# One tile, one copy and one subtraction for the silu products of both token tiles in the FFNs of a decoder trunk

## The chip, the cores and the metric

The kernel runs on one core of one Trainium2 chip. Its time is the device time of one execution in microseconds, and a kernel's time is the median over its runs. A profile shows one execution, taken by the hardware profiler.

## The reference

A decoder trunk of two layers over 256 tokens of width 1024, all in float32. Each layer has two SwiGLU FFNs with 2816 hidden columns, a pair of token mixers between them, three layer norms, and a gated embedding (PLE) at the end:

```python
def swiglu(x, w_gate, w_up, w_down):
    return (jax.nn.silu(x @ w_gate) * (x @ w_up)) @ w_down

def reference(x, p, ...):
    for i in range(DEPTH):
        x = layer_norm(DN_ALPHA * x + 0.5 * swiglu(x, ffn_w_gate[i, 0], ffn_w_up[i, 0], ffn_w_down[i, 0]),
                       ln_g[i, 0], ln_b[i, 0])
        if i % 2 == 0:
            mix = mixer_ab(...)
        else:
            mix = mixer_cd(...)
        x = layer_norm(DN_ALPHA * x + mix, ln_g[i, 1], ln_b[i, 1])
        x = layer_norm(DN_ALPHA * x + 0.5 * swiglu(x, ffn_w_gate[i, 1], ffn_w_up[i, 1], ffn_w_down[i, 1]),
                       ln_g[i, 2], ln_b[i, 2])
        x = x + jax.nn.sigmoid(x @ ple_w_gate[i]) * (p[i] @ ple_w_proj[i])
    return x
```

## The kernel before

The 256 tokens are two tiles (`NT`) of 128. The FFNs are called f00 and f01 (layer 0) and f10 and f11 (layer 1). Behind f00 come layer norm 0, mixer_ab (its first projection writes `pj_u`) and layer norm 1; behind f01 layer norm 2 and PLE0, then f10; behind f10 layer norm 3 and mixer_cd (first projection `pj_hq`); behind f11 layer norm 5 and PLE1, which ends the kernel.

Every product is split: an operand is held as a rounded part (`...h`, type fp32r) and a remainder (`...l`), and `mm3` (L70, L71, L72) issues three matmuls, wh with xh, wl with xh, wh with xl. So weights pass through three steps: SyncE loads a unit of 1 MB into `wst`, ScalarE casts half of it to `wh` (L61), VectorE subtracts to get `wl` (L62). An activation that changes from tokens-by-features to features-by-tokens is transposed by TensorE into PSUM (tag `tr`, two buffers), cast by ScalarE and subtracted by VectorE: `xh` and `xl` (L112, L113) for layer norms and PLE, `hh` and `hl` (L212, L213) inside the FFN.

An FFN goes through 11 slices of 256 hidden columns. `gate_up(f)` is 48 matmuls into two PSUM tiles `gu`, one for each token tile; `hidden(f)` makes silu(gate) times up (`sg`, L205 and L206), transposes it (`ht`, L209) and splits it; `down(f)` is 24 matmuls into four accumulators `acc_<FFN>_<token tile>_<half of 1024 columns>`. The down matmuls of slices 9 and 10 stand in a last loop over the token tiles, with the layer norm of the tile right behind its own:

```python
    for t in range(NT):
        for n in range(2):
            for f in (NF - 2, NF - 1):
                down(f, t, hs[f], ds[f], (n,))
        layer_norm(g, ln, t, acc[t], 0.5 / ALPHA, xT)
```

`layer_norm` is a chain on VectorE: L126 (`r_ln`, a half of 512 columns at a time) with statistics behind each half, small operations, L136 and L138 (`x_ln`) by halves; then TensorE transposes (`tp_ln`, L142) and `xh`, `xl` follow. PLE's projection (`pps`, copied to `pp`) needs no layer norm; its gate (`acc_ple`) does. During f00 hooks prepare S5 parameters (`s5w`, `s5k` through `tr`, `s5pe` copies at L546, L553 and L558). At the end of f00 ScalarE's queue also issues the loads of mixer_ab: `nw_dt` (L593, cast at L597), `abrow` (L764), and W, tab, T, Q from `s5d` (L671 to L677), twice. At the end of f10 it issues `nw_glr` (L593, cast at L597) and `gup`.

The program names dependencies, not an order. Tile's scheduler (`schedule_with_timeline_sim=True`) lays out the order of each engine's instructions with a cost model of its own; `behind` adds an edge that keeps one instruction after another on the same engine.

Of the kernel before, what the change touches and what calls it, by code (L numbers as in the profile page):

```python
# [33 lines left out]
def f32(ap):  # L34
    return ap.bitcast(F32)
# [81 lines left out]
def layer_norm(g, n, t, acc, coef, xT):  # L117

    nc = g.nc
    name = f"ln{n}_{t}"  # L120
    r = g.lnp.tile([P, D], F32, tag="ln_r", name=f"r_{name}")
    st = g.small.tile([P, 2, 6], F32, tag="ln_st", name=f"st_{name}")
    half = [slice(512 * h, 512 * h + 512) for h in range(2)]
    for h in range(2):
        s = half[h]
        op = nc.vector.scalar_tensor_tensor(r[:, s], acc[h], coef, g.x[t][:, s], op0=ALU.mult, op1=ALU.add)  # L126
        if t:
            behind(g, op, g.scaled)
        nc.vector.bn_stats(st[:, h, :], r[:, s])
    mv = g.small.tile([P, 2], F32, tag="ln_mv", name=f"mv_{name}")  # L130
    nc.vector.bn_aggr(mv, st.rearrange("p a b -> p (a b)"))
    rstd = rsqrt(g, mv[:, 1:2], 1, EPS / (ALPHA * ALPHA), 1.0, name)
    x = g.xp.tile([P, D], F32, tag=f"x{t}", name=f"x_{name}")
    for h in range(2):
        s = half[h]
        nc.vector.scalar_tensor_tensor(r[:, s], r[:, s], mv[:, 0:1], g.grow[n][0][:, s], op0=ALU.subtract,  # L136
                                       op1=ALU.mult)
        op = nc.vector.scalar_tensor_tensor(x[:, s], r[:, s], rstd, g.grow[n][1][:, s], op0=ALU.mult, op1=ALU.add)  # L138
        g.scaled = (op.ins,)
        tp = g.ps.tile([P, 4, P], F32, tag="tr", name=f"tp_{name}_{h}", bufs=2)  # L140
# [17 lines left out]
def acc_tiles(g, name):  # L158
    return [[g.ps.tile([P, 512], F32, tag="acc", name=f"acc_{name}_{t}_{h}", bufs=4) for h in range(2)]
            for t in range(NT)]  # L160


def run_tiles(g, ps, xT, tile_major=False):

    nc = g.nc

    def part(kh, t, pieces):
        for j in range(4):
            k = 4 * kh + j
            wh, wl = pieces[j // 2]  # L170
            c = slice(512 * (j % 2), 512 * (j % 2) + 512)
            mm3(nc, ps[t], *of_tile(xT, t, k), wh[:, c], wl[:, c], k == 0, k == KT - 1)

    if tile_major:
        units = [g.w.unit() for kh in range(2)]
        for t in range(NT):
            for kh in range(2):
                part(kh, t, units[kh])
        return
    for kh in range(2):  # L180
        pieces = g.w.unit()
        for t in range(NT):
            part(kh, t, pieces)
# [8 lines left out]
def ffn_body(g, name, ln, hooks, hp, wx):  # L192
    nc = g.nc
    acc = acc_tiles(g, name)

    def gate_up(f):
        ps = [g.ps.tile([P, 512], F32, tag="mm", name=f"gu_{name}_{f}_{t}", bufs=2) for t in range(NT)]
        run_tiles(g, ps, g.xT, tile_major=f == 0)
        return ps

    def hidden(f, ps):
        out = []
        for t in range(NT):
# [12 lines left out]

    def down(f, t, h, pieces, cols=(0, 1)):
        hh, hl = h[t]
        for n in cols:
            for k in range(2):  # L220
                wh, wl = pieces[k]
                c = slice(512 * n, 512 * n + 512)
                mm3(nc, acc[t][n], hh[:, k, :], hl[:, k, :], wh[:, c], wl[:, c],
                    f == 0 and k == 0, f == NF - 1 and k == 1)

    ps = gate_up(0)
    if -1 in hooks:
        hooks[-1]()
    hs, ds = {}, {}
    for f in range(NF):  # L230
        hs[f] = hidden(f, ps)
        if f + 1 < NF:
            ps = gate_up(f + 1)
        for d in DOWNS[f]:
            ds[d] = g.w.unit(wx if d >= NF - 2 else None)
            if d < NF - 2:
                for t in range(NT):
                    down(d, t, hs[d], ds[d])
        if f in hooks:
            hooks[f]()  # L240
    xT = new_xT(g, f"{name}")
# [5 lines that stand above are left out]
    g.xT = xT  # L247
# [1270 lines left out]
```

## Time and profile before

| | |
|---|---|
| median of 3 runs | 1237.29 us (1236.95 to 1238.12) |
| profiled execution, its own time | 1236.71 us |
| its span | 1234.9 us |
| mean granted TensorE clock | 0.996 |
| TensorE busy | 97% of the span |
| VectorE, ScalarE busy | 69%, 50% |

The time of an execution is its span and a little around it. Shares of busy time are averages over the whole span. [...]

### The profile page before, as it was taken

What the parts mean: (1) busy time and instruction counts of PE and PEld (TensorE: products, weight loads), DVE (VectorE), ACT (ScalarE), POOL (GpSimd) and SP (SyncE); (2) the same over time, 40 slices, a digit from 0 to 9 for tenths busy, and PEclk for the clock granted to TensorE, in tenths of its full rate; (3) what the DMA queues carried; (4) which work ended last, traced back from release to release, by engine and by line L of the source; (5) the groups of instructions that cost most, each with busy time, mean ns of one, the idle gap of its engine ahead of it and who ended that gap; (6) DMA issues with size and microseconds to landing.
All of it is one profiled execution on the core that took longest, in us unless ns stands there. A gap on an engine that the chain in (4) does not pass through costs nothing.

```text
span 1234.9 us, 16234 instructions
## 1 busy us (share of the span) xinstructions
PE 1202.8 (97%) x6274; PEld 1011.3 (82%) x6274; DVE 848.5 (69%) x1353; ACT 621.1 (50%) x944; POOL 48.5 (4%) x78
## 2 busy tenths in 40 slices
PE   6999999899999999999999999999999899999998
PEld 4888788699997878888887888887888778888886
DVE  6998874779879876555567554546689776545466
ACT  6566765444535635444536444443575535444434
POOL 0000000020101000000000000000100010000000
PEclk9999999999999999999999999999999999999999
DMA  7676778687842647555535655554633227555532
GB/s 267 218 253 241 248 259 320 219 289 263 278 140 72 222 143 254 177 198 180 195 137 204 217 192 186 189 190 165 227 122 137 103 80 255 185 193 182 197 144 102
DMA packets 40797, 242.12 MB, mean 196 GB/s; under 512 B 4848, under 2 KB 5520, under 8 KB 17040
## 3 DMA queue, kind: packets, MB, share of 16 engines
q1 hardware_dynamic: 30672, 206.06, 48.2%
q0 software_dynamic: 3952, 18.88, 4.3%
q10 hardware_dynamic: 6096, 16.16, 3.9%
q8 instruction: 49, 0.80, 0.3%
q14 instruction: 28, 0.23, 0.1%
HBM read 224.30 MB, written 16.78 MB: 195 GB/s over the span
## 4 chain that ended last, share of the span: by engine, by line
PE 72%; issue 5%; DVE 3%; DMA 1%; POOL 0%; ACT 0%; DVEq 0%; ACTq 0%; POOLq 0%
PE gu_f L72 10%; PE gu_f L71 10%; PE gu_f L70 9%; PE acc_f L72 5%; PE acc_f L70 5%; PE acc_f L71 5%; PE acc_ple L71 1%; PE acc_ab L70 1%; PE acc_ab L72 1%; PE acc_ab L71 1%; PE acc_ple L72 1%; PE acc_ple L70 1%; PE ht_f L209 1%; PE lv_h L1140 1%; PE lv_g L1140 1%
## 5 line engine op out<-in xcount | busy, mean ns | idle before, releaser
L62 DVE TENSOR_TENSOR wl<-wst,wh 128x1024 fp32r<-128x1024 f32 (+1 forms) x378 | 453.6, 1216 | 269.2 <-ACT wh L61 262.7
L61 ACT CAST wh<-wst 128x1024 fp32r<-128x1024 f32 (+1 forms) x378 | 386.7, 1045 | 319.8 <-PE gu_f L72 108.0
L70 PE MATMUL acc_f<-wh,hh_f 128*128 128x512 f32 x352 | 137.4, 391 | 1.2 <-ACT hh_f L212 1.2
L71 PE MATMUL acc_f<-wl,hh_f 128*128 128x512 f32 x352 | 137.7, 391 | 0.0
L72 PE MATMUL acc_f<-wh,hl_f 128*128 128x512 f32 x352 | 136.3, 392 | 0.2 <-DVE hl_f L213 0.2
L70 PEld LDWEIGHTS acc_f<-wh,hh_f 128*128 128x128 f32 x352 | 66.1, 188 | 15.4 <-ACT hh_f L212 2.1
L72 PEld LDWEIGHTS acc_f<-wh,hl_f 128*128 128x128 f32 x352 | 66.1, 188 | 14.1 <-DVE hl_f L213 0.7
L71 PEld LDWEIGHTS acc_f<-wl,hh_f 128*128 128x128 f32 x352 | 66.1, 188 | 13.5
L70 PE MATMUL gu_f<-wh,xh_in 128*128 128x512 f32 x176 | 70.9, 408 | 5.9 <-ACT wh L61 5.9
L205 ACT ACTIVATE sg_f<-gu_f 128x256 f32<-128x256 f32 x88 | 33.7, 384 | 75.1 <-PE gu_f L72 73.3
L70 PE MATMUL gu_f<-wh,xh_ple 128*128 128x512 f32 x176 | 69.7, 396 | 1.6 <-ACT xh_ple L112 1.6
L71 PE MATMUL gu_f<-wl,xh_in 128*128 128x512 f32 x176 | 70.7, 403 | 0.0
L70 PE MATMUL gu_f<-wh,xh_cd 128*128 128x512 f32 x176 | 69.8, 396 | 0.5 <-ACT xh_cd L112 0.5
L70 PE MATMUL gu_f<-wh,xh_ab 128*128 128x512 f32 x176 | 69.7, 396 | 0.5 <-ACT xh_ab L112 0.5
L72 PE MATMUL gu_f<-wh,xl_in 128*128 128x512 f32 x176 | 70.1, 399 | 0.0
L72 PE MATMUL gu_f<-wh,xl_ab 128*128 128x512 f32 x176 | 69.0, 392 | 0.7 <-DVE xl_ab L113 0.7
L72 PE MATMUL gu_f<-wh,xl_cd 128*128 128x512 f32 x176 | 69.0, 392 | 0.7 <-DVE xl_cd L113 0.7
L71 PE MATMUL gu_f<-wl,xh_cd 128*128 128x512 f32 x176 | 68.8, 391 | 0.2 <-DVE wl L62 0.2
L71 PE MATMUL gu_f<-wl,xh_ab 128*128 128x512 f32 x176 | 68.8, 391 | 0.2 <-DVE wl L62 0.2
L72 PE MATMUL gu_f<-wh,xl_ple 128*128 128x512 f32 x176 | 68.7, 392 | 0.0
L71 PE MATMUL gu_f<-wl,xh_ple 128*128 128x512 f32 x176 | 68.6, 390 | 0.0
L206 DVE TENSOR_TENSOR sg_f<-sg_f,gu_f 128x256 f32<-128x256 f32 x88 | 36.5, 416 | 27.2 <-ACT sg_f L205 27.2
(470 smaller groups left out, 2397.0 us busy)
## 6 DMA issues: line engine op xcount, KB each, us to landing
wst<-in_wall_dram SPq DMA_DIRECT2D x185, 1024.0 KB, 4.9
s5d<-s5pk POOLq DMA_DIRECT2D x8, 896.0 KB, 4.7
s5d<-s5pe POOLq DMA_DIRECT2D x8, 768.0 KB, 3.8
row<-in_lnr_dram SPq DMA_DIRECT2D x12, 512.0 KB, 6.4
W<-s5d ACTq DMA_DIRECT2D x8, 512.0 KB, 6.5
Q<-s5d ACTq DMA_DIRECT2D x8, 512.0 KB, 5.5
tab<-s5d ACTq DMA_DIRECT2D x8, 384.0 KB, 3.8
wst<-in_wall_dram SPq DMA_DIRECT2D x4, 512.0 KB, 6.4
```

The source lines that it names most:

```text
L61: ops = [nc.scalar.copy(wh[:, c], src[:, c])]
L62: ops.append(nc.vector.tensor_tensor(wl[:, c], src[:, c], f32(wh[:, c]), op=ALU.subtract))
L70: nc.tensor.matmul(out, xh, wh, start=first, stop=False)
L71: nc.tensor.matmul(out, xh, wl, start=False, stop=False)
L72: nc.tensor.matmul(out, xl, wh, start=False, stop=last)
L205: nc.scalar.activation(sg, ps[t][:, 0:256], AF.Silu)
L206: nc.vector.tensor_tensor(sg, sg, ps[t][:, 256:512], op=ALU.mult)
L209: nc.tensor.transpose(tp[:, k, :], sg[:, k * P:(k + 1) * P], g.ident)
L1140: nc.tensor.matmul(lp[0:m, n * t + j], xt[:, 0:m], xt.rearrange("p (a s b) -> p a s b", s=2, b=b)[:, :, 1, :], start=True, stop=True)
```

## The change

`hidden` holds both token tiles in one tile each: `sg` [128, 2, 256] with one buffer (it was one tile for each token tile, two buffers), `ht` [128, 2, 2, 128] in one `tr` buffer (it was one for each token tile), and `hh`, `hl` with three buffers as before. The two silu activations and the two products still go token tile by token tile. The four transposes follow in a fixed order, tile 1 first; one cast and one subtraction over 512 columns split all of it. `down` is as it was, on slices of the new tiles. `g.hidden` is used nowhere else. In the changed kernel lines behind L201 have numbers higher by up to 3 (L207 for L205, L215 for the cast and subtraction).

```diff
--- before.py
+++ after.py
@@ -199,20 +199,22 @@
         return ps
 
     def hidden(f, ps):
-        out = []
+        sg = hp.tile([P, NT, 256], F32, tag="sg", name=f"sg_{name}_{f}", bufs=1)
+        tp = g.ps.tile([P, NT, 2, P], F32, tag="tr", name=f"ht_{name}_{f}", bufs=2)
+        hh = hp.tile([P, NT, 2, P], F32R, tag="hh", name=f"hh_{name}_{f}", bufs=3)
+        hl = hp.tile([P, NT, 2, P], F32R, tag="hl", name=f"hl_{name}_{f}", bufs=3)
         for t in range(NT):
-            sg = hp.tile([P, 256], F32, tag="sg", name=f"sg_{name}_{f}_{t}")
-            nc.scalar.activation(sg, ps[t][:, 0:256], AF.Silu)
-            nc.vector.tensor_tensor(sg, sg, ps[t][:, 256:512], op=ALU.mult)
-            tp = g.ps.tile([P, 2, P], F32, tag="tr", name=f"ht_{name}_{f}_{t}", bufs=2)
+            nc.scalar.activation(sg[:, t], ps[t][:, 0:256], AF.Silu)
+            nc.vector.tensor_tensor(sg[:, t], sg[:, t], ps[t][:, 256:512], op=ALU.mult)
+        last = ()
+        for t in reversed(range(NT)):
             for k in range(2):
-                nc.tensor.transpose(tp[:, k, :], sg[:, k * P:(k + 1) * P], g.ident)
-            hh = hp.tile([P, 2, P], F32R, tag=f"hh{t}", name=f"hh_{name}_{f}_{t}", bufs=3)
-            hl = hp.tile([P, 2, P], F32R, tag=f"hl{t}", name=f"hl_{name}_{f}_{t}", bufs=3)
-            nc.scalar.copy(hh, tp)
-            nc.vector.tensor_tensor(hl, tp, f32(hh), op=ALU.subtract)
-            out.append((hh, hl))
-        return out
+                op = nc.tensor.transpose(tp[:, t, k, :], sg[:, t, k * P:(k + 1) * P], g.ident)
+                behind(g, op, last)
+                last = (op.ins,)
+        ops = [nc.scalar.copy(hh, tp), nc.vector.tensor_tensor(hl, tp, f32(hh), op=ALU.subtract)]
+        g.hidden = tuple(op.ins for op in ops)
+        return [(hh[:, t], hl[:, t]) for t in range(NT)]
 
     def down(f, t, h, pieces, cols=(0, 1)):
         hh, hl = h[t]
```

ScalarE and VectorE each have 44 instructions fewer; TensorE has as many as before. The scheduler's order changes in many places. Three of them follow, without the numbers that stand ahead of the rows.

TensorE at the end of f10, the last rows of the FFN before the transposes of layer norm 3. A name is the tile, then FFN, token tile and column half, and `hh_f10_10` is slice 10. Before:

```order
L72 MATMUL acc_f10_1_1_6250<-wh_130_0_7549,hl_f10_9_1_7420 128x512
L70 MATMUL acc_f10_1_1_6250<-wh_130_1_7553,hh_f10_9_1_7419 128x512
L71 MATMUL acc_f10_1_1_6250<-wl_130_1_7554,hh_f10_9_1_7419 128x512
L72 MATMUL acc_f10_1_1_6250<-wh_130_1_7553,hl_f10_9_1_7420 128x512
L70 MATMUL acc_f10_1_1_6250<-wh_131_0_7559,hh_f10_10_1_7509 128x512
L71 MATMUL acc_f10_1_1_6250<-wl_131_0_7560,hh_f10_10_1_7509 128x512
L72 MATMUL acc_f10_1_1_6250<-wh_131_0_7559,hl_f10_10_1_7510 128x512
L70 MATMUL acc_f10_1_1_6250<-wh_131_1_7563,hh_f10_10_1_7509 128x512
L71 MATMUL acc_f10_1_1_6250<-wl_131_1_7564,hh_f10_10_1_7509 128x512
L72 MATMUL acc_f10_1_1_6250<-wh_131_1_7563,hl_f10_10_1_7510 128x512
L142 MATMUL tp_ln3_0_0_7608<-cs_209,x_ln3_0_7605 128x128 x4
L142 MATMUL tp_ln3_0_1_7617<-cs_209,x_ln3_0_7605 128x128 x4
```

After:

```order
L71 MATMUL acc_f10_0_1_6116<-wl_131_1_7366,hh_f10_10_7303 128x512
L72 MATMUL acc_f10_0_1_6116<-wh_131_1_7365,hl_f10_10_7304 128x512
L72 MATMUL acc_f10_1_0_6117<-wh_131_0_7361,hl_f10_10_7304 128x512
L70 MATMUL acc_f10_1_0_6117<-wh_131_1_7365,hh_f10_10_7303 128x512
L71 MATMUL acc_f10_1_0_6117<-wl_131_1_7366,hh_f10_10_7303 128x512
L72 MATMUL acc_f10_1_0_6117<-wh_131_1_7365,hl_f10_10_7304 128x512
L72 MATMUL acc_f10_1_1_6118<-wh_131_0_7361,hl_f10_10_7304 128x512
L70 MATMUL acc_f10_1_1_6118<-wh_131_1_7365,hh_f10_10_7303 128x512
L71 MATMUL acc_f10_1_1_6118<-wl_131_1_7366,hh_f10_10_7303 128x512
L72 MATMUL acc_f10_1_1_6118<-wh_131_1_7365,hl_f10_10_7304 128x512
L142 MATMUL tp_ln3_0_0_7410<-cs_209,x_ln3_0_7407 128x128 x4
L142 MATMUL tp_ln3_0_1_7419<-cs_209,x_ln3_0_7407 128x128 x4
```

Before, the last rows are all of `acc_f10_1_1`, and the last row of token tile 0 stands 24 matmuls ahead of `tp_ln3_0_0`; now slice 10 is run for all four accumulators, and the last row of token tile 0 (`acc_f10_0_1`) stands 8 matmuls ahead of `tp_ln3_0_0`.

ScalarE at the end of f00, from the loads of mixer_ab to the casts of layer norm 0's first token tile (`DMA` rows are issues of transfers). Before:

```order
L593 DMA nw_dt_2423<-in_abdt_dram 128x128
L671 DMA W_0_2448<-s5d0_87 128x1024
L673 DMA tab_0_2450<-s5d0_87 128x768
L597 CAST nws_dt_2425<-nw_dt_2423 128x8x16
L675 DMA T_0_2452<-s5d0_87 128x512
L677 DMA Q_0_2454<-s5d0_87 128x1024
L764 DMA abrow_2499<-in_abrow_dram 128x48
L671 DMA W_1_2528<-s5d1_88 128x1024
L112 CAST xh_f00_2078<-tp_ln0_0_0_2119 128x4x128
L673 DMA tab_1_2530<-s5d1_88 128x768
L112 CAST xh_f00_2078<-tp_ln0_0_1_2128 128x4x128
```

After (the issues of `nw_dt` and `abrow` stand just ahead):

```order
L599 CAST nws_dt_2359<-nw_dt_2357 128x8x16
L774 ACT_TABLE_LOAD
L774 ACTIVATE A_2458<-abrow_2433 128x16
L673 DMA W_0_2382<-s5d0_87 128x1024
L675 DMA tab_0_2384<-s5d0_87 128x768
L677 DMA T_0_2386<-s5d0_87 128x512
L679 DMA Q_0_2388<-s5d0_87 128x1024
L673 DMA W_1_2462<-s5d1_88 128x1024
L675 DMA tab_1_2464<-s5d1_88 128x768
L677 DMA T_1_2466<-s5d1_88 128x512
L679 DMA Q_1_2468<-s5d1_88 128x1024
L112 CAST xh_f00_2012<-tp_ln0_0_0_2053 128x4x128
```

The activation of `abrow` with its table load, which stood seven rows behind the first `xh_f00` cast, and three more of the W, tab, T, Q issues now stand ahead of it.

VectorE at the end of f01, from layer norm 2 of token tile 1 to the subtraction for weight unit 95, PLE0's first. Before:

```order
L126 SCALAR_TENSOR_TENSOR r_ln2_1_5967<-acc_f01_1_0_4568,x_ln1_1_4532 128x512
L126 SCALAR_TENSOR_TENSOR r_ln2_1_5967<-acc_f01_1_1_4569,x_ln1_1_4532 128x512
L129 BN_STATS st_ln2_1_5968<-r_ln2_1_5967 128x6 x2
L131 BN_AGGR mv_ln2_1_5973<-st_ln2_1_5968 128x2
L79 TENSOR_SCALAR rs_w_ln2_1_5975<-mv_ln2_1_5973 128x1
L136 SCALAR_TENSOR_TENSOR r_ln2_1_5967<-r_ln2_1_5967,mv_ln2_1_5973,row0_2_4553 128x512 x2
L138 SCALAR_TENSOR_TENSOR x_ln2_1_5979<-r_ln2_1_5967,rs_r_ln2_1_5977,row1_2_4555 128x512
L113 TENSOR_TENSOR xl_f01_5887<-tp_ln2_0_0_5927,xh_f01_5886 128x4x128
L138 SCALAR_TENSOR_TENSOR x_ln2_1_5979<-r_ln2_1_5967,rs_r_ln2_1_5977,row1_2_4555 128x512
L113 TENSOR_TENSOR xl_f01_5887<-tp_ln2_0_1_5936,xh_f01_5886 128x4x128
L62 TENSOR_TENSOR wl_95_0_6059<-wst_95_6056,wh_95_0_6058 128x1024
```

After:

```order
L126 SCALAR_TENSOR_TENSOR r_ln2_1_5835<-acc_f01_1_0_4502,x_ln1_1_4466 128x512
L126 SCALAR_TENSOR_TENSOR r_ln2_1_5835<-acc_f01_1_1_4503,x_ln1_1_4466 128x512
L129 BN_STATS st_ln2_1_5836<-r_ln2_1_5835 128x6
L113 TENSOR_TENSOR xl_f01_5755<-tp_ln2_0_0_5795,xh_f01_5754 128x4x128
L129 BN_STATS st_ln2_1_5836<-r_ln2_1_5835 128x6
L113 TENSOR_TENSOR xl_f01_5755<-tp_ln2_0_1_5804,xh_f01_5754 128x4x128
L131 BN_AGGR mv_ln2_1_5841<-st_ln2_1_5836 128x2
L79 TENSOR_SCALAR rs_w_ln2_1_5843<-mv_ln2_1_5841 128x1
L136 SCALAR_TENSOR_TENSOR r_ln2_1_5835<-r_ln2_1_5835,mv_ln2_1_5841,row0_2_4487 128x512 x2
L62 TENSOR_TENSOR wl_95_0_5927<-wst_95_5924,wh_95_0_5926 128x1024
```

The two `xl_f01` rows, which stood behind the layer norm of token tile 1, moved between its statistics; `wl_95_0` stands right behind the scaling pass (L136), ahead of the `x_ln2_1` rows rather than behind them.

## Rows read from the trace of the kernel before

**Rows 1.** The page: each engine's busy us, share of the span, instructions.

```profile
PE 1202.8 (97%) x6274; PEld 1011.3 (82%) x6274; DVE 848.5 (69%) x1353; ACT 621.1 (50%) x944; POOL 48.5 (4%) x78
```

**Rows 2.** TensorE's waits over the whole span: us in total, times, longest.

```profile
PE ht_f L209 <- DVE sg_f L206: 4.6, 1, 4.6
...
PE acc_f L70 <- ACT hh_f L212: 1.2, 2, 0.8
...
PE acc_f L72 <- DVE hl_f L213: 0.2, 1, 0.2
```

**Rows 3.** The page's costliest groups: busy us, mean ns of one, idle before.

```profile
L62 DVE TENSOR_TENSOR wl<-wst,wh 128x1024 fp32r<-128x1024 f32 (+1 forms) x378 | 453.6, 1216 | 269.2 <-ACT wh L61 262.7
L61 ACT CAST wh<-wst 128x1024 fp32r<-128x1024 f32 (+1 forms) x378 | 386.7, 1045 | 319.8 <-PE gu_f L72 108.0
```

**Rows 4.** Four lines by form: duration ns min/median/max, first and last start.

```profile
L212 ACT CAST hh_f<-ht_f x88: 347/368/383, 25.9 to 1191.7; 128x256 fp32r<-128x256 f32 x88
...
L213 DVE TENSOR_TENSOR hl_f<-ht_f,hh_f x88: 410/417/426, 27.7 to 1192.1; 128x256 fp32r<-128x256 f32 x88
...
L112 ACT CAST xh_f<-tp_ln x16: 586/596/641, 227.9 to 1208.5; 128x512 fp32r<-128x512 f32 x16
...
L113 DVE TENSOR_TENSOR xl_f<-tp_ln,xh_f x16: 633/680/692, 228.6 to 1209.9; 128x512 fp32r<-128x512 f32 x16
```

**Rows 5.** TensorE's timeline in slice 6 of f00: start us, us, then idle before.

```profile
150.25 0.50 PE L70 MATMUL acc_f<-wh,hh_f 128*128 128x512 f32 x1 [0.76 <-ACT hh_f L212]
150.59 0.40 PE L71 MATMUL acc_f<-wl,hh_f 128*128 128x512 f32 x1
150.82 0.40 PE L70 MATMUL acc_f<-wh,hh_f 128*128 128x512 f32 x1
```

**Rows 6.** TensorE's timeline at the end of f00.

```profile
226.35 1.29 PE L142 MATMUL tp_ln<-cs,x_ln 128*128 128x128 f32 x8 [1.90 <-DVE x_ln L138]
228.53 0.50 PE L70 MATMUL pj_u<-wh,xh_f 128*128 128x512 f32 x1 [0.89 <-ACT xh_f L112]
```

**Rows 7.** ScalarE's timeline at the end of f00; ACTq is its issuing of DMAs.

```profile
224.26 0.34 ACTq L593 DMA_DIRECT2D nw_dt<-in_abdt_dram  x1
...
226.06 0.30 ACT L597 CAST nws_dt<-nw_dt 128x128 fp32r<-128x128 f32 x1 [5.37 <-DMA nw_dt<-in_abdt_dram]
...
226.44 0.44 ACTq L677 DMA_DIRECT2D Q<-s5d  x1
...
227.89 0.59 ACT L112 CAST xh_f<-tp_ln 128x512 fp32r<-128x512 f32 x1 [1.53 <-PE tp_ln L142]
```

**Rows 8.** Line 764, the load of abrow: from issue to landing.

```profile
DMA to landing us min/median/max: 7.6/7.6/7.6
```

**Rows 9.** TensorE's timeline at the end of f01.

```profile
646.08 1.03 PE L142 MATMUL tp_ln<-cs,x_ln 128*128 128x128 f32 x8
...
650.90 0.50 PE L71 MATMUL acc_ple<-wl,xh_f 128*128 128x512 f32 x1
```

**Rows 10.** VectorE's timeline at the end of f01.

```profile
638.12 0.69 DVE L126 SCALAR_TENSOR_TENSOR r_ln<-acc_f,x_ln 128x512 f32<-128x512 f32 x1 [1.30 <-PE acc_f L72]
...
641.21 1.41 DVE L138 SCALAR_TENSOR_TENSOR x_ln<-r_ln,rs_r_ln,row 128x512 f32<-128x512 f32 x2
```

**Rows 11.** TensorE's timeline at the end of f10.

```profile
861.76 1.03 PE L142 MATMUL tp_ln<-cs,x_ln 128*128 128x128 f32 x8
...
864.70 0.50 PE L72 MATMUL pj_hq<-wh,xl_f 128*128 128x512 f32 x1 [0.94 <-DVE xl_f L113]
```

**Rows 12.** ScalarE's timeline at the end of f10.

```profile
866.40 0.30 ACT L597 CAST nws_glr<-nw_glr 128x128 fp32r<-128x128 f32 x1 [1.04 <-DMA nw_glr<-in_cdlr_dram]
```

**Rows 13.** TensorE's timeline between PLE0 and f10.

```profile
675.31 0.50 PE L70 MATMUL gu_f<-wh,xh_ple 128*128 128x512 f32 x1 [1.64 <-ACT xh_ple L112]
```

**Rows 14.** Two stretches: us, busy time of each engine, PEclk, DMA share, GB/s.

```profile
24.30:27.40 3.10, 3.06 (x9) 2.48 (x10) 3.10 (x11) 1.96 (x3) 0.00 (x0) 0.51 0.78 317
226.00:228.00 2.00, 1.25 (x8) 0.83 (x8) 2.00 (x5) 0.41 (x2) 0.00 (x0) 1.00 0.79 284
```

## The prediction

> **What bounds the kernel now.** I read the busy shares first: TensorE is busy 97% of a span of 1234.9 us, VectorE 69% and ScalarE half [rows 1]. So a microsecond counts only where TensorE stands still, and the list of TensorE's waits comes next. Of the whole kernel's FFN work only these waits touch what the change edits: 4.6 us before the first slice's transposes (f00, slice 0, where the silu product is late), 1.2 us in two pieces before a down matmul that needs `hh`, and 0.2 us for `hl` [rows 2]. All of them lie in f00. In f01, f10 and f11, 33 of the 44 slices, TensorE never waits for `hidden()`. VectorE and ScalarE, on the other hand, spend their idle time waiting for each other and for TensorE: the weight subtractions `wl` wait 262.7 us for the casts `wh`, and the casts 108.0 us for the gate-and-up matmuls that free their tiles [rows 3]. A shorter evacuation therefore only lengthens waits that already exist.
>
> **The part the diff shows.** Per slice one 128x512 cast replaces two of 368 ns, and one 128x512 subtraction replaces two of 417 ns [rows 4]. The new shapes stand elsewhere in this trace, PSUM to SBUF with the same types: 596 and 680 ns [rows 4]. So ScalarE saves 2 x 368 - 596 = 140 ns and VectorE 2 x 417 - 680 = 154 ns a slice; times 44 that is 6.2 and 6.8 us. Neither is on TensorE's path. What covers them is the 16.6 us of matmuls that a slice gives TensorE (72 at the 0.23 us between two starts [rows 5]). I take 0; the bounds are 0 and -6.8, the latter if VectorE set the pace everywhere. The four transposes are the same four. Their cost is not changed by being issued in a row.
>
> [...]
>
> **What else moves.** One token tile can no longer run ahead of the other inside a slice, and each slice takes one `tr` buffer instead of two. The scheduler lays out all engines anew around that. I compared both orders and price each place where a row that TensorE waits for moved.
>
> *f00, middle: -1.2.* In slice 6 TensorE waits 0.76 us for `hh` [rows 5] and 0.24 us for `hl` [rows 2]; each restart costs about 0.1 more (the first matmul lasts 0.50). In the new order the transposes of slice 6 stand some 26 matmuls ahead of its down matmuls, 5.9 us, so both waits go. Bounds -1.2 and 0.
>
> *f00, end: +4.6.* Now `tp_ln` starts at 226.35 and the projection `pj_u` at 228.53 [rows 6]. After, the single cast of slice 10 must wait for all four transposes, with three s5pe copies ahead of it on ScalarE (0.3 us each), so down 10 starts about 1.1 us later; and the accumulators of tile 0 end 8 matmuls before those of tile 1 instead of 24. That puts `tp_ln` at about 227.9. The larger thing is ScalarE's own queue. Now the cast of `nw_dt` runs at 226.06 once its DMA, issued at 224.26, has landed, and `xh` starts at 227.89 [rows 7]. After, `abrow` is loaded before that cast, and the table load and the activation of `abrow`, then all eight W/tab/T/Q issues (about 0.44 us each, 3.6 in all), stand ahead of `xh`. With the last matmul 1.1 us later, `nw_dt` is issued at about 225.3 and `abrow` at 225.8. `abrow` took 7.6 us to land [rows 8], but with big transfers issued ahead of it; `nw_dt`, with none ahead, took 1.8. I take 3, nearer the latter: activation at 228.8, issues until 232.4, `xh` done at 233.0, `pj_u` at 233.1, which is 4.6 later. Bounds: 1.8 and 7.6 for `abrow` give +3.4 and +9.2; if the issues cost ScalarE's compute nothing, only the 1.6 of `tp_ln` are left.
>
> *f01, end: +4.3.* Now all of tile 0's down matmuls end 24 + 12 matmuls before `tp_ln` at 646.08, and its LN chain (from `r_ln` 638.12 to the first half of `x_ln` at 641.21 + 0.74) is hidden; the first L71 of `acc_ple` starts at 650.90 [rows 9, 10]. After, tile 0 ends 12 matmuls before tile 1 and its transposes stand behind 6 pps matmuls more, at about 647.5, still without a wait. But ScalarE then has a pp copy, `xh`, a pp copy, `xh` and only after these the cast of weight 95: the second transposes end at 649.8 (647.5 and 6 matmuls and two groups of transposes), the copy at 650.1, `xh` 0.6 later and the cast [rows 3] at 651.7. VectorE, in its turn, has `r_ln` of tile 1, `xl`, statistics and the scaling pair ahead of `wl_95_0`: `xl` of the second half ends at 651.4, the two L136 passes 1.40 later, with the small operations at 653.1, and the subtraction (1.22 [rows 3]) at 654.3. L71 starts there. TensorE has by then done 8 transposes more than at 650.90, 0.9 us, so the same point lies at 650.0 before: +4.3. [...]
>
> *f11, end: +4.3.* [...]
>
> *f10, end: +3.4.* Tile 0's last matmul moves from 24 to 8 before the end. Now `tp_ln` follows at 861.76 without a wait and the first L72 of `pj_hq` at 864.70 [rows 11]. After, the chain (4.3 us from the last matmul of tile 0 to half an `x_ln`, and 0.5 because both halves come together) puts `tp_ln` at 859.7 + 4.8 = 864.5. And the cast of `nw_glr`, which waits for its DMA until 866.40 [rows 12], now stands ahead of `xh`: 866.7 + 0.6 + 0.68 = 868.0 for `xl`, so L72 is 3.4 late. Without that DMA about +2.2; at most +5.
>
> *PLE0 into f10: -1.8.* TensorE waits 1.64 us at 675.31 for `xh_ple` [rows 13], because ScalarE has a weight cast ahead of it whose tile the last `acc_ple` matmuls free. In the new order the weight cast stands behind `xh_ple`. Bounds -0.5 (the wait passes to the next weight) and -2.1.
>
> *Tail: +0.4.* The last gate pieces of tile 0 (0.69 us, as `r_ln` in [rows 10]) come closer to those of tile 1. *Clock: +0.8.* [...] After the 1.90 us idle ahead of `tp_ln` at 226.35 it stays at 1.00 [rows 6, 14]. [...]
>
> **Sum.** -1.2 + 4.6 + 4.3 + 4.3 + 3.4 - 1.8 + 0.4 + 0.8 = +14.8 on the profiled execution's 1236.71 us (span 1234.9 and 1.8 around it): 1251.5. The median of the runs shown, 1237.29, is 0.6 above that execution, so I say 1252.
>
> **The rivals.**
> *The ends are cheaper (1243).* The order is as printed but ScalarE's issues and casts hide behind landing transfers: f00 +1.6, f01 and f11 +1.9 each, f10 +2.2, the stalls -3.0, the tail +0.4: +5.0 to +6, so 1242 to 1244. For it: the issue rows lie in ScalarE's sequencer beside running casts [rows 7]. Against: an `xh` behind them in the order cannot be started first.
> *Faster (1234).* The two stalls go (-3.0) and the ends stay hidden. It is decided by whether the LN chain at the three t-major ends still fits under TensorE's matmuls: at f10 it has 8 x 0.23 = 1.8 us of cover for a 4.8 us chain, so it wins only if the ends cost under 0.5 us together.
> *Faster by cheaper evacuation (1231).* If VectorE or ScalarE set the pace in the slices, up to 6.8 us come back. Against: of the waits for their results only those of f00 exist [rows 2]. [...]
> *No change (1237).* Stalls saved and ends lost cancel: ends of 2 to 5.5 us in all.
> [...]
>
> **How the numbers follow.** Chances: the forecast (1247 to 1257) 0.60, cheaper ends (1240 to 1247) 0.17, worse 0.10, no change 0.07, the two faster ones 0.04 and 0.02. About 0.2% (2.5 us) is what a measurement of this kernel can tell from no change; so slower 0.86, same 0.08, faster 0.06. From 1242 to 1260 leaves out the faster ones, no change, and half of the worse.
>
> **What would show it.** In the new profile: ScalarE with 44 casts of about 590 ns and VectorE with 44 subtractions of about 680; no wait for `hh` near 150; `pj_u` waiting for `xh_f` some 4 us at the end of f00; `acc_ple` L71 waiting for `wl` twice, 2 to 3 us; `tp_ln` waiting about 3 us at the end of f10; no wait for `xh_ple`. I am wrong if TensorE's idle time does not rise by about 10 us or more, or if it rises inside the slices instead of at the ends.

## The result and the profile after

The changed kernel takes 1254.84 us in the median of four runs (1253.58 to 1256.09), the kernel before 1237.12 beside it: a ratio of 1.0136, interval 1.0123 to 1.0148, 17 us slower. The forecast was 1252, between 1242 and 1260. The profiled execution took 1254.29 us.

The page's first lines, the span, and each engine's busy us with its share and its instructions [rows 1]:

```profile
span 1252.5 us, 16123 instructions
...
PE 1210.8 (97%) x6274; PEld 1019.7 (81%) x6274; DVE 845.3 (67%) x1309; ACT 620.1 (50%) x900; POOL 50.4 (4%) x78
```

ScalarE and VectorE are a little less busy, TensorE 8.0 us more with the same instructions, and the span is 17.6 us longer. The span is TensorE's busy time and its idle time: idle time grew by 9.6 us (32.1 to 41.7), busy time by the other 8.0. Busy time contains what TensorE does at half speed (PEclk 0.50 to 0.61 behind the four ends, below), so not all of the loss is waiting.

TensorE's waits over the whole span: us in total, times, longest [rows 2]:

```profile
PE tp_ln L142 <- DVE x_ln L138: 5.7, 3, 2.7
PE acc_ple L71 <- DVE wl L62: 4.1, 2, 2.0
PE gu_f L70 <- DVE sg_f L208: 3.9, 1, 3.9
...
PE acc_ple L70 <- ACT wh L61: 3.3, 2, 1.7
PE pj_u L70 <- ACT xh_f L112: 3.0, 2, 2.7
PE acc_f L70 <- ACT hh_f L215: 1.5, 1, 1.5
...
PE gu_f L70 <- ACT xh_ple L112: 0.5, 1, 0.5
```

The waits in f00's slice 6, 0.76 us for `hh` [rows 5] and 0.24 for `hl` [rows 2], are gone; between 30 and 214 us there is no wait at all. The rest of the 1.2 us for `hh` of [rows 2] stood ahead of slice 10's down matmuls, and this wait grew to 1.5 us (`acc_f`). What is new stands at the ends: `tp_ln` waits three times, `acc_ple` four times (twice for a weight's cast, twice for its subtraction), `pj_u` twice, 3.0 us in all. Apart from the one behind f00's first slice, there before too (`sg_f`, 3.9 us for 4.6 before), and the 1.5 us for `hh`, no wait for what `hidden` makes lies inside the slices.

The merged cast and subtraction by form [rows 4]: duration ns min/median/max, then the first and the last start.

```profile
L215 ACT CAST hh_f<-ht_f x44: 563/581/588, 30.0 to 1203.4; 128x512 fp32r<-128x512 f32 x44
L215 DVE TENSOR_TENSOR hl_f<-ht_f,hh_f x44: 682/685/693, 30.6 to 1204.1; 128x512 fp32r<-128x512 f32 x44
```

581 and 685 ns stand for 2 x 368 and 2 x 417. That is 155 and 149 ns less a slice. Operations that follow each other overlap a little (below, two casts of 0.59 us take 1.07 at 230.42), so the engines' busy times fall by less, 1.0 and 3.2 us against [rows 1].

The end of f00. TensorE first: start us, us, and in brackets the idle time and who ended it [rows 6]:

```profile
223.56 0.39 PE L72 MATMUL acc_f<-wh,hl_f 128*128 128x512 f32 x1
226.56 1.75 PE L142 MATMUL tp_ln<-cs,x_ln 128*128 128x128 f32 x8 [2.62 <-DVE x_ln L138]
231.06 0.80 PE L70 MATMUL pj_u<-wh,xh_f 128*128 128x512 f32 x1 [2.75 <-ACT xh_f L112]
```

ScalarE there (ACTq rows are issues of transfers) [rows 7, 8]:

```profile
223.38 0.45 ACTq L766 DMA_DIRECT2D abrow<-in_abrow_dram  x1
...
225.10 1.28 ACT L774 ACT_TABLE_LOAD   x1
226.41 0.22 ACT L774 ACTIVATE A<-abrow 128x16 f32<-128x16 f32 x1
226.49 0.34 ACTq L673 DMA_DIRECT2D W<-s5d  x1
...
229.91 0.47 ACTq L679 DMA_DIRECT2D Q<-s5d  x1
230.42 1.07 ACT L112 CAST xh_f<-tp_ln 128x512 fp32r<-128x512 f32 x2 [3.79 <-DMA W<-s5d]
```

`tp_ln` waits for the layer norm 2.62 us, and `pj_u` then 2.75 for `xh`. The casts start at 230.42, right behind the eighth issue (229.91). The sequence is as worked out: `abrow`, issued at 223.38, has landed by 226.41, the issues run from 226.49 for 3.9 us, and then come the casts. The activation's table load ends at 226.38, the moment at which `abrow` lands, 3.0 us behind its issue; so the activation would not have started earlier had `abrow` landed sooner.

The end of f01, TensorE and then VectorE [rows 9, 10]:

```profile
652.27 0.60 PE L142 MATMUL tp_ln<-cs,x_ln 128*128 128x128 f32 x4
654.54 0.49 PE L70 MATMUL acc_ple<-wh,xh_f 128*128 128x512 f32 x1 [1.67 <-ACT wh L61]
657.08 0.64 PE L71 MATMUL acc_ple<-wl,xh_f 128*128 128x512 f32 x1 [2.05 <-DVE wl L62]
```

```profile
653.57 0.69 DVE L113 TENSOR_TENSOR xl_f<-tp_ln,xh_f 128x512 fp32r<-128x512 f32 x1 [0.47 <-ACT xh_f L112]
...
654.49 1.40 DVE L136 SCALAR_TENSOR_TENSOR r_ln<-r_ln,mv_ln,row 128x512 f32<-128x512 f32 x2
655.81 1.22 DVE L62 TENSOR_TENSOR wl<-wst,wh 128x1024 fp32r<-128x1024 f32 x1
```

TensorE waits for `wh_95` and, one matmul later, for `wl_95`, whose subtraction (655.81) stands behind the second `xl`, the statistics and the scaling pair. f11 has the same two waits.

The end of f10, TensorE and ScalarE [rows 11, 12]:

```profile
869.46 0.39 PE L72 MATMUL acc_f<-wh,hl_f 128*128 128x512 f32 x1
872.50 1.94 PE L142 MATMUL tp_ln<-cs,x_ln 128*128 128x128 f32 x8 [2.66 <-DVE x_ln L138]
874.85 0.79 PE L70 MATMUL pj_hq<-wh,xh_f 128*128 128x512 f32 x1 [0.41 <-ACT xh_f L112]
```

```profile
874.01 0.30 ACT L599 CAST nws_glr<-nw_glr 128x128 fp32r<-128x128 f32 x1 [12.66 <-DMA nw_glr<-in_cdlr_dram]
```

`tp_ln` lasts 1.94 us for 8 transposes, where the same group took 1.03 in [rows 11]: TensorE is at half speed already when it starts (PEclk 0.50 from 872.4, below). The cast of `nw_glr` still ends just ahead of `xh`.

The granted clock behind the four ends: us, then busy time of each engine, PEclk, DMA share, GB/s [rows 14]:

```profile
231.00:234.00 3.00, 2.94 (x7) 2.32 (x8) 2.96 (x5) 2.39 (x4) 0.00 (x0) 0.50 1.02 377
657.00:661.00 4.00, 3.92 (x12) 3.19 (x13) 2.48 (x4) 0.25 (x1) 0.00 (x0) 0.57 0.31 59
872.40:879.00 6.60, 6.09 (x18) 4.80 (x19) 6.59 (x11) 3.16 (x5) 0.00 (x0) 0.50 0.09 32
1223.00:1227.00 4.00, 3.93 (x13) 3.21 (x14) 2.62 (x5) 0.59 (x1) 0.00 (x0) 0.61 0.27 57
```

PEclk, the third number from the right, is 0.50 to 0.61 in all four. Before, it was 1.00 at the end of f00 [rows 14], and also from 640 to 690 and from 860 to 880 us.

### The profile page after: what moved, and what is told of

Read it like the earlier page. It is cut to its first block, busy times and chain, and to the rows that moved or that the text cites. A ratio compares the mean times of both kernels' runs of the same rounds, so it can differ in the third digit from the quotient of the medians.

```text
span 1252.5 us, 16123 instructions
## 1 busy us (share of the span) xinstructions
PE 1210.8 (97%) x6274; PEld 1019.7 (81%) x6274; DVE 845.3 (67%) x1309; ACT 620.1 (50%) x900; POOL 50.4 (4%) x78
## 4 chain that ended last, share of the span: by engine, by line
PE 90%; DVE 4%; DMA 3%; ACT 2%; issue 1%; ACTq 0%; POOL 0%; SPq 0%; DVEq 0%
PE gu_f L72 12%; PE gu_f L70 12%; PE gu_f L71 12%; PE acc_f L72 6%; PE acc_f L71 6%; PE acc_f L70 6%; DMA wst<-in_wall_dram 2%; PE ht_f L212 2%; PE acc_ab L70 1%; PE acc_ab L72 1%; PE acc_ab L71 1%; PE s5v L684 1%; PE s5k L553 1%; PE s5y L707 1%; DVE wl L62 1%; PE lv_h L1142 1%
## 5 line engine op out<-in xcount | busy, mean ns | idle before, releaser
L71 PE MATMUL acc_f<-wl,hh_f 128*128 128x512 f32 x352 | 137.2, 390 | 0.0
L72 PE MATMUL acc_f<-wh,hl_f 128*128 128x512 f32 x352 | 134.6, 390 | 0.0
L71 PEld LDWEIGHTS acc_f<-wl,hh_f 128*128 128x128 f32 x352 | 66.1, 188 | 13.7
L72 PEld LDWEIGHTS acc_f<-wh,hl_f 128*128 128x128 f32 x352 | 66.1, 188 | 13.6
L71 PE MATMUL gu_f<-wl,xh_in 128*128 128x512 f32 x176 | 70.7, 403 | 0.0
L72 PE MATMUL gu_f<-wh,xl_in 128*128 128x512 f32 x176 | 70.7, 402 | 0.0
L72 PE MATMUL gu_f<-wh,xl_ab 128*128 128x512 f32 x176 | 69.4, 395 | 0.7 <-DVE xl_ab L113 0.7
L72 PE MATMUL gu_f<-wh,xl_ple 128*128 128x512 f32 x176 | 69.6, 395 | 0.5 <-DVE xl_ple L113 0.5
L72 PE MATMUL gu_f<-wh,xl_cd 128*128 128x512 f32 x176 | 69.5, 395 | 0.3 <-DVE xl_cd L113 0.3
L71 PE MATMUL gu_f<-wl,xh_ab 128*128 128x512 f32 x176 | 68.8, 391 | 0.2 <-DVE wl L62 0.2
L71 PE MATMUL gu_f<-wl,xh_cd 128*128 128x512 f32 x176 | 68.8, 391 | 0.0
L71 PE MATMUL gu_f<-wl,xh_ple 128*128 128x512 f32 x176 | 68.7, 390 | 0.0
L207 ACT ACTIVATE sg_f<-gu_f 128x256 f32<-128x256 f32 x88 | 33.6, 383 | 65.7 <-PE gu_f L72 63.8
```

The source lines that it names most:

```text
L207: nc.scalar.activation(sg[:, t], ps[t][:, 0:256], AF.Silu)
```

## The experiments

Each experiment ran in five rounds against the kernel before on the same chip. Ratios are to that kernel. It took 1237.12 us beside the changed kernel, 1237.86 beside kernels 1 to 4, 1238.83 beside 5 to 8 and 1238.65 beside 9 and 10, so the us of different groups compare only to a us or two; the ratios do without that.

| kernel | median us | ratio | interval |
|---|---|---|---|
| changed kernel | 1254.84 | 1.0136 | 1.0123 to 1.0148 |
| 1 last slice apart | 1236.20 | 0.9989 | 0.9980 to 0.9997 |
| 2 only last slice joint | 1254.67 | 1.0133 | 1.0118 to 1.0149 |
| 3 tile-major tail | 1239.23 | 1.0016 | 1.0003 to 1.0029 |
| 4 casts first on ScalarE | 1252.21 | 1.0112 | 1.0098 to 1.0125 |
| 5 TensorE kept busy | 1251.18 | 1.0103 | 1.0088 to 1.0117 |
| 6 casts apart, transposes joint | 1245.75 | 1.0063 | 1.0048 to 1.0079 |
| 7 products first | 1246.83 | 1.0062 | 1.0050 to 1.0074 |
| 8 combined | 1234.04 | 0.9957 | 0.9944 to 0.9970 |
| 9 before, with edges | 1234.36 | 0.9970 | 0.9959 to 0.9982 |
| 10 all joint, with edges | 1242.13 | 1.0029 | 1.0017 to 1.0042 |

**1 and 2: which slices cost?** The theory is that of the prediction: the loss sits at the FFN ends. The rival is that every joint slice costs a little. In 1, `hidden` transposes and splits slice 10 by token tile again, into the same `hh` and `hl`; 2 has the condition the other way round.

```diff
     def hidden(f, ps):
...
+        if f == NF - 1:        # 2: if f < NF - 1:
+            for t in range(NT):
+                (silu, product, transposes into an own tp, cast to hh[:, t], subtraction to hl[:, t])
+            return [(hh[:, t], hl[:, t]) for t in range(NT)]
```

Kernel 1: 

> The changed kernel, but slice 10 of each FFN (4 of the 44 slices) transposes, casts and subtracts each token tile by itself again. Theory (the loss sits at the FFN ends, where the joint cast of slice 10 lets tile 0 finish late): about 1236 us, 1234 to 1238, since the 40 joint slices cost TensorE nothing and the 1.2 us stall of slice 6 in f00 stays away. Rival (each joint slice costs a little, both tiles and one transpose buffer being coupled): 10/11 of the loss stays, about 1253 us.

Kernel 2: 

> The reverse: only slice 10 of each FFN is joint, the other 40 slices are as before the change. Theory (loss at the FFN ends): the whole loss, 1254 to 1257 us, with the waits of TensorE at the same four places as in the changed kernel. Rival (each joint slice costs a little): 1/11 of the loss, about 1239 us.

Forty joint slices give 0.9989, four give 1.0133. The four last slices make the whole loss, and the other forty none. Three of kernel 2's waits of TensorE (columns as above):

```profile
PE tp_ln L142 <- DVE x_ln L138: 5.6, 3, 2.7
...
PE acc_ple L71 <- DVE wl L62: 4.1, 2, 2.0
...
PE acc_ple L70 <- ACT wh L61: 3.3, 2, 1.7
```

They match the changed kernel's to 0.1 us. The wait at the fourth place, 2.75 us of `pj_u` for `xh` at the end of f00, is not there:

```profile
228.06 1.75 PE L142 MATMUL tp_ln<-cs,x_ln 128*128 128x128 f32 x8 [2.60 <-DVE x_ln L138]
229.50 0.79 PE L70 MATMUL pj_u<-wh,xh_f 128*128 128x512 f32 x1
```

In kernel 2 the first `xh` cast (228.87) starts ahead of the last issue. Its last down matmul of f00 starts later, at 225.07 for 223.56 in the changed kernel, with PEclk 0.50 from 218.2 to 221.5 ahead of it (1.00 there in the changed kernel). So the total is the same, and the ends of f01, f10 and f11 are, but f00 loses its time in another way than the expectation said.

**3: TensorE's order.** All slices are joint; an edge keeps tile 1's last down matmuls behind tile 0's.

```diff
                 a, b = mm3(...)        # first and last matmul
+                if f >= NF - 2:
+                    if t:
+                        behind(g, a, tail)
+                    else:
+                        tail[:] = [b.ins]
```

> The changed kernel with every slice joint; in the last loop an edge keeps token tile 1's down matmuls of slices 9 and 10 behind all of token tile 0's, so that tile 0 ends 24 matmuls ahead of tile 1 again. Theory (it is the order of TensorE's down matmuls that takes the cover from the layer norm): most of the loss comes back, 1237 to 1242 us; a few us may stay at the ends of f01 and f11, where ScalarE still has all four projection copies ahead of the casts. Rival (the joint cast itself is late, and TensorE waits for it wherever it stands): over 1248 us, with new waits for hh_f at the ends.

1.0016: nearly all of the loss is gone. The joint cast is not late: TensorE's wait for `hh` is the same single 1.5 us in f00 as in the changed kernel. What is left at the end of f01, TensorE's timeline:

```profile
646.42 1.04 PE L142 MATMUL tp_ln<-cs,x_ln 128*128 128x128 f32 x8
649.17 0.50 PE L70 MATMUL acc_ple<-wh,xh_f 128*128 128x512 f32 x1 [1.72 <-ACT wh L61]
```

`tp_ln` no longer waits; 1.72 us remain for `wh`, as expected, because ScalarE still has the projection copies ahead. The edge moved more than TensorE's order: at the end of f00 one of the eight issues now stands ahead of the first `xh` cast (224.97, the cast at 225.41). What kernel 3 shows is the order of the down matmuls together with what the scheduler makes of it on the other engines.

**4: ScalarE's order.** TensorE's order is that of the changed kernel. `g.t0` is tile 0's last `xh` cast of the layer norm.

```diff
-    nc.scalar.dma_start(W, ...)                 # tab, T, Q alike
+    op = nc.scalar.dma_start(W, ...)
+    behind(g, op, g.t0 if b < 2 else ())
...                                             # and the activation of abrow, the casts of nw
+    behind(g, op, g.t0)
```

> The changed kernel with the same order on TensorE; on ScalarE edges put the casts xh of token tile 0 ahead of the eight W, tab, T, Q issues and of the activation of abrow at the end of f00, and ahead of the cast of nw_glr at the end of f10. Theory (ScalarE's queue holds the casts back): the projection behind f00 starts about 2.0 us earlier, when its transposes end, and the one behind f10 about 0.8 us: 1252 us, 1251 to 1253. Rival (the issues lie beside the casts and hold nothing back): 1254.8 within 1 us.

1.0112, some 3 us of the 17. The interval overlaps a little with that of the changed kernel, but all four runs (1250.0 to 1252.6) lie under all four of kernel 2 on the same chip (1253.5 to 1255.7). The end of f00 in this kernel:

```profile
222.85 0.39 PE L72 MATMUL acc_f<-wh,hl_f 128*128 128x512 f32 x1
225.86 1.94 PE L142 MATMUL tp_ln<-cs,x_ln 128*128 128x128 f32 x8 [2.62 <-DVE x_ln L138]
227.62 0.80 PE L70 MATMUL pj_u<-wh,xh_f 128*128 128x512 f32 x1
```

`pj_u` follows the transposes without a wait, 4.8 us behind the last down matmul rather than 7.5. The wait for the layer norm is unchanged, and `tp_ln` takes 1.94 us, where 8 transposes at a clock of 1.00 took 1.03 in [rows 11].

**5: the clock.** Unused float32 matmuls fill the new idles; the orders are otherwise those of the changed kernel.

```diff
+def warm(g, name, n, after=()):
+    ps = g.ps.tile([P, 512], F32, tag="mm", name=f"warm_{name}", bufs=2)
+    for _ in range(n):
+        op = g.nc.tensor.matmul(ps[:, 0:384], g.cst("strict"), g.cst("mask3"), start=True, stop=True)
+        behind(g, op, after)
+        after = (op.ins,)
```

> The changed kernel plus 18 matmuls whose result is used nowhere (128 by 384, float32, into a spare PSUM tile): five between the last down matmul and the first layer norm transposes at the ends of f00 and f10, four between the second layer norm transposes and acc_ple at the ends of f01 and f11, where TensorE idles. All other orders are unchanged. Theory (each new idle lowers the granted clock to half for a stretch, worth 1.0 to 1.6 us at each of the four places): TensorE stays at full speed behind f10 and f00 at least, and 2.5 to 5 us come back, 1250 to 1252 us. Rival (the half-speed stretches lie beside waits and cost nothing): 1254.8 within 1 us, or more if the added matmuls are in the way.

1.0103 against 1.0136, about 4 us back (0.7 to 7 by the ends of the two intervals). The same four places:

```profile
231.60:234.60 3.00, 2.95 (x7) 2.33 (x8) 2.97 (x5) 2.38 (x4) 0.00 (x0) 0.50 0.90 337
657.00:661.00 4.00, 2.60 (x13) 1.72 (x12) 4.00 (x6) 0.52 (x1) 0.72 (x1) 1.00 0.00 0
872.80:879.30 6.50, 5.59 (x27) 4.06 (x26) 6.49 (x10) 3.17 (x5) 0.00 (x0) 1.00 0.10 36
1221.00:1225.00 4.00, 2.60 (x10) 1.57 (x9) 4.00 (x6) 0.90 (x1) 0.92 (x1) 1.00 0.00 0
```

Three are at full speed now; behind f00, where the wait for `xh` of some 3 us is not filled, the clock is still 0.50. TensorE at the end of f10:

```profile
870.12 3.39 PE L190 MATMUL warm_f<-cs 128*128 128x384 f32 x10
873.34 1.04 PE L142 MATMUL tp_ln<-cs,x_ln 128*128 128x128 f32 x8
```

The five matmuls (ten records) fill 3.4 us where 2.66 were idle, so they hold `tp_ln` up; yet it takes 1.04 us rather than 1.94. That is not all that half speed costs at these three places, for this kernel pays elsewhere. Behind f00 PEclk is 0.50 until 237.8 us, and in the changed kernel only until 234.0. And there is a new stretch, with no wait ahead of it (from 958.0 to 961.4 TensorE is busy all the time at 1.00):

```profile
961.50:964.90 3.40, 3.40 (x8) 2.73 (x9) 3.40 (x8) 1.36 (x3) 0.00 (x0) 0.50 0.59 164
```

The profiled execution, 1253.22 us, is the slowest of the four (1249.10 is the fastest), so the others may lack some of this.

**6 and 7: what holds tile 0 back in slice 10?** In 6 the transposes of slice 10 go tile 0 first and each tile has its own cast; in 7 all is joint, and both products stand ahead of the next three weight units.

```diff
 6
+        if f == NF - 1:
+            for t in range(NT):
+                nc.scalar.copy(hh[:, t], tp[:, t])
+                nc.vector.tensor_tensor(hl[:, t], tp[:, t], f32(hh[:, t]), op=ALU.subtract)
 7
+        if f == NF - 1:
+            for n in range(1, 4):
+                g.w.behind[g.w.at + n] = (a.ins, b.ins)     # silu and product of tile 1, the last
```

Kernel 6: 

> The changed kernel, but in slice 10 of each FFN the four transposes, still into one tile and in a fixed order, go tile 0 first, and each token tile has its own cast and subtraction. In the scheduler's order tile 0 then ends 12 matmuls ahead of the end at f10 and 8 at f00. Theory (what delays tile 0 is that its transposes wait for tile 1's product, not the width of the cast): most of the loss stays, 1246 to 1253 us. Rival (the 128x512 cast and subtraction are what delays tile 0): 1236 to 1239 us.

Kernel 7: 

> The changed kernel; edges put both silu products of slice 10 ahead of the casts and subtractions of the three weight units that follow it on ScalarE and VectorE. In the scheduler's order tile 0 then ends 14 matmuls ahead of the end at f10, 14 and 12 projection matmuls ahead at f01 and f11, and 8 as before at f00. Theory (tile 1's product stands behind four weight subtractions, and joint transposes pass that on to tile 0): f01 and f11 get most of their loss back, f10 about half, f00 none, 1241 to 1246 us. Rival (the lateness has another source, slice 10's own matmuls): over 1250 us.

Both bring about half back (1.0063, 1.0062). In us kernel 6 lies 0.3 under its range and kernel 7 0.8 above; taken by the ratios from the 1237.12 of the changed kernel's round, kernel 6 (1244.9) lies 1.1 under and kernel 7 (1244.8) inside. Kernel 7's waits came place by place as expected: at f00 `tp_ln` still waits 2.6 us, at f01 the waits for `wh` and `wl` are 0.3 and 0.4 (1.7 and 2.0 in the changed kernel), and f10 has half. The wait of `tp_ln` at the end of f10 in 6 and in 7 (2.7 in the changed kernel):

```profile
PE tp_ln L142 <- DVE x_ln L138: 2.2, 2, 1.8
```

```profile
PE tp_ln L142 <- DVE x_ln L138: 1.9, 2, 1.3
```

In 6 tile 0 ends 12 matmuls ahead of the end, in 7 it is 14, in the changed kernel 8, and the wait falls as that grows. The wide cast alone is not the cause, since 6 has narrow ones; nor is the place of the products alone. Kernel 6 changes the order of the transposes as well, so it does not price the narrow casts by themselves.

**8 to 10: is there a faster version?** 8 is kernel 1 with the edges of 3 and 4. 9 is the kernel before with both edges, 10 the changed kernel with both.

Kernel 8: 

> Joint slices 0 to 9, slice 10 by token tile, tile 1's last down matmuls kept behind tile 0's, and the casts xh of tile 0 ahead of the issues on ScalarE. Theory (the stall of slice 6 and the uncovered layer norm behind f00 are independent, 1.2 and about 2.5 us): 1233 to 1235 us, faster than both kernels. Rival (what is won behind f00 is lost to the next wait in mixer_ab): 1236 to 1237.

Kernel 9: 

> The kernel before the change, no slice joint, with the same two sets of edges as the combined kernel (tile 1's last down matmuls behind tile 0's, the casts xh of tile 0 ahead of ScalarE's issues). If the combined kernel's gain comes from the end of f00 alone: 1234 to 1235 us, no different from it. If the joint slices 0 to 9 bring their own 1 to 2 us (the stall of slice 6 and its like in f00): 1235 to 1236.5, slower than the combined kernel by that.

Kernel 10: 

> The changed kernel, all slices joint, with both sets of edges. Theory (with the order of the ends repaired, what stays of the loss is ScalarE's four projection copies ahead of the casts at f01 and f11, 1.7 us of waiting each): 1236 to 1239 us, 3 to 4 slower than the combined kernel. Rival (the joint cast of slice 10 costs nothing once the order stands): 1233 to 1235.

8 and 9 are faster than the kernel before, 0.9957 and 0.9970, and their intervals overlap: the gain comes from the end of f00, and whether the joint slices 0 to 9 add 1 us is not settled. The end of f00 in kernel 8:

```profile
221.83 0.39 PE L72 MATMUL acc_f<-wh,hl_f 128*128 128x512 f32 x1
222.06 1.03 PE L142 MATMUL tp_ln<-cs,x_ln 128*128 128x128 f32 x8
223.34 0.50 PE L70 MATMUL pj_u<-wh,xh_f 128*128 128x512 f32 x1 [0.24 <-ACT xh_f L112]
```

The layer norm is covered: from the last down matmul to `pj_u` 1.5 us, where the kernel before has 4.5. The execution shown, 1229.53 us, is the fastest of kernel 8's six and the one with the highest mean clock (0.998; the others have 0.994 or 0.995). Kernel 10 came out 3 us above the expected range, and above kernel 3, with which it shares TensorE's order at all four ends. By the ratios it is 1.6 us above kernel 3, and the intervals overlap. One visible difference is the clock behind f01, in kernel 10 and then in kernel 3:

```profile
651.00:655.00 4.00, 3.98 (x12) 2.82 (x11) 4.00 (x5) 2.70 (x4) 0.00 (x0) 0.57 0.27 51
```

```profile
649.00:653.00 4.00, 3.80 (x18) 2.69 (x19) 4.00 (x6) 3.86 (x6) 0.00 (x0) 1.00 0.00 0
```

Both have a wait of 1.72 us for `wh` ahead of this. Kernel 3's own runs spread from 1236.4 to 1245.9 us, with granted clocks from 0.997 to 0.990. The two profiled executions are 4.6 us apart, and of that 3.4 is TensorE's busy time (1208.0 and 1204.6) and 1.2 its idle time: between these two it is mostly half speed. Whether an order makes the clock fall more often in kernel 10 stays open.

## Why the prediction held, step by step

Starts of the same matmuls before and after, from TensorE's timelines, with the difference:

| start of | before | after | difference |
|---|---|---|---|
| last down matmul of f00 | 224.06 | 223.56 | -0.5 |
| first matmul of f01 | 455.17 | 458.20 | +3.0 |
| first matmul of f10 | 675.31 | 682.92 | +7.6 |
| first matmul of f11 | 1012.60 | 1024.48 | +11.9 |
| last matmul | 1229.77 | 1247.09 | +17.3 |

**Inside the slices: 0, as said.** Kernel 1 shows it. The saving of 150 ns a slice went into waits that ScalarE and VectorE had anyway. They are 50% and 67% busy in the changed kernel, and TensorE got nothing of it back.

**f00, middle: -1.2 said, -0.5 measured at the end of f00.** The stall of slice 6 is gone and the first wait is 0.7 us shorter (3.88 for 4.61), but behind it TensorE ran at half speed until 29.0 us rather than 27.4, and the longer wait ahead of down 10 (+1.0, priced under the next step) lies in this row too.

**f00, end: +4.6 said, about +3.5 with the clock.** ScalarE's queue was right, and 3 us from `abrow`'s issue to its activation too (3.0), though the table load, which the sum left out, ends at the same moment: that the sum came out without it is luck. The 1.1 us by which I put down 10 later are there as a wait, 1.49 us for 0.46; TensorE was 1.4 us ahead by then, so down 10 started a little before its old time. From the last down matmul to `pj_u` it is 7.5 us for 4.5, +3.0 where +3.5 was said (4.6 less the 1.1). Middle and end together: +3.4 said, +3.0 measured. Kernel 4 prices ScalarE's order at f00 and f10 together at 3 us.

**f01 end and PLE0 into f10: 4.3 - 1.8 = +2.5 said, +4.6 measured.** ScalarE's chain alone, which the rival of the cheaper ends takes, gave +1.9: the cast of weight 95 done at 651.7 and one matmul of 0.2, against 650.0. The end of f01 lost 1.67 + 2.05 = 3.7 us of idle time to the two waits, and by the starts of the matmuls about 4.1, near the 4.3 priced. Both ends of that difference were put some 1.5 us too late, since six matmuls of `pps` run ahead of slice 10's last down matmuls now (640.92 to 642.06); the difference hardly feels it. Two sizes were off. The half speed behind it costs 4.0 x 0.43 = 1.7 (the second of the four windows). And the waits between PLE0 and f10 did not go: 1.64 and 0.15 became 0.52 for `xh_ple` and 0.46 for `xl_ple`. ScalarE's rows show why:

```profile
679.90 2.00 ACT L61 CAST wh<-wst 128x1024 fp32r<-128x1024 f32 x2 [3.23 <-DMA wst<-in_wall_dram]
...
682.29 1.06 ACT L112 CAST xh_ple<-tp_ple 128x512 fp32r<-128x512 f32 x2
```

The prediction had the weight cast that was in the way behind `xh_ple`; two other weight casts stand ahead of it, and they had to wait 3.23 us for their DMA. With 0.98 us of waits in place of 1.79 the step brings 0.8, near the bound of 0.5 that I had given for another reason.

**f10, end: +3.4 said, +4.3 measured,** of it 2.8 ahead of `tp_ln` (872.50 - 869.46, less one matmul). The first L72 of `pj_hq`, which I had priced, starts 6.4 us behind the last down matmul (875.87), and before it was 3.2: +3.2 where +3.4 was said. Behind it 7 matmuls start 0.43 us apart instead of 0.23, +1.4.

**f11 and tail: +4.3 + 0.4 said, +5.4 and 0.3 measured.** The +4.3 is that of f01: before, the first L71 of `acc_ple` starts at 1208.34, 557.4 us behind f01's, and the new order is the same. The two waits are those of f01, about 4.1; half speed makes most of the rest. The tail is the time from the last matmul to the end of the span, 5.1 before and 5.4 after.

**The mis-sized term is the clock.** I took 0.8 us, an estimate of mine: half of the 1.5 us that the 3.1 us at 0.51 behind the 4.6 us wait in f00 cost [rows 2, 14]. No run shows a term of that size; the changed kernel showed a fall at all four ends in its place, with PEclk 0.50 to 0.61. Behind the matmul that the last wait holds back it cost 1.5, 1.7, 1.4 and 1.6 us by the four windows and the starts at f10, about 6 together. TensorE's busy time, 8.0 us more, is an upper bound, since some of the slow work lies beside waits: at f10 `tp_ln` lasts 0.9 us longer, but `xh` had to wait for the cast of `nw_glr` all the same. My reason for the 0.8 was that the new idles at f01, f10 and f11, which I had estimated at 2.4 to 3.0 us, lay between one that was followed by half speed (4.6 [rows 2, 14]) and one that was not (1.90 [rows 6, 14]). Kernel 5 fills three of them: there PEclk is 1.00 instead of 0.57, 0.50 and 0.61, and about 4 us come back.

With four falls of 1.5 us my sum would have been about 1257. The waits at the ends were close (+3.0 for 3.5, +4.1 for 4.3 twice, +3.2 for 3.4), and the step into f10 brought 1.0 us less than said. What keeps the time under 1257 are smaller differences that I had not priced, some 2 us in all behind the ends, such as a wait of 0.39 us of `pj_hq` for `wl` that is gone; they are not traced one by one. So the places and the order of events were right, and that 1252 lies as near as 3 us to 1254.84 is in part luck. "A microsecond counts only where TensorE stands still", the prediction's first step, left out work at half speed.

The cause is shown by kernels 1 to 3: slice 10's joint transposes make the scheduler run slice 9's down matmuls for both tiles ahead of slice 10's, so tile 0 no longer ends 24 matmuls early, and the layer norm chain (4.9 us at f10 in the changed kernel, from tile 0's last matmul at 867.64 to `tp_ln` at 872.50) loses its cover. Kernel 3 restores that order with all slices joint, and kernel 1 by taking slice 10 apart. Why the scheduler places the joint transposes as late as it does was only narrowed down (6 and 7: tile 1's product and the shared tile each bear a part), not settled.

## What to carry to other kernels

Here an edit that saves instructions on engines with slack (50% and 67% busy) was worth nothing in the slices. Where such an edit joins two independent tiles, it can cost at the place where one tile was used to run ahead: look at the last iteration and at the chain behind the loop, not at the steady state. Under a scheduler, compare the two orders at each boundary and price what stands ahead of the critical instruction on every engine, issues of transfers included. When an idle appears, add what TensorE may lose at half speed behind it; here that was about 6 us over four ends.

## What was unexpected of the hardware

Half speed followed waits shorter than the 4.6 us that I had seen it follow [rows 2, 14]. `tp_ln` at the end of f10 ran slow behind 2.66 us of idle (1.94 us for 1.03); `acc_ple` behind 1.67 and 2.05 with one matmul between (PEclk 0.57). Behind 1.72 us kernel 10 fell to 0.57 and kernel 3 stayed at 1.00 at the same place. Behind the 3.37 us ahead of `o_g` the kernel before fell to 0.50 (983.6 to 986.6), and kernels 6 and 8 stayed at 1.00. In kernel 5 the clock fell to 0.50 at 961.5 with no wait ahead of it. In these runs the length of one wait alone did not tell whether the clock fell.

`abrow` landed 7.6 us after its issue with `nw_dt` and four large transfers issued ahead of it [rows 8], and 3.0 us after it with only `nw_dt` ahead. The other traces agree: 7.3 us in kernel 1, which has the old order, 2.9 or 3.0 in the eight kernels with only `nw_dt` ahead and at least 1.8 us to the next issue behind, and 4.4 in kernel 7, where the first large one is issued 0.6 us behind it. Here the order of issues on ScalarE's queue moved the landing of this 24 KB transfer by over 4 us.
